# Layer 2's input weights split during layer 1's MLP and kept in DRAM scratch

## The chip, the cores and the metric

The kernel runs on one core of a Trainium2 chip. The metric is the device time of one execution in microseconds (us). The engines are TensorE (PE, with its weight loads PEld), VectorE (DVE), ScalarE (ACT), GpSimd (POOL) and SyncE (SP), which issues nearly all DMAs from one in-order queue.

## The reference

A decoder trunk of two layers on 512 tokens of width 1024, float32. Each layer is

```
h = rmsnorm(x, g_mix[l])
cq, ckv, kr, aq, ak, av, qi, ki, wi, rq, rk, rv, rg = split(h @ w_in[l])
A: latent attention, 8 heads; q from cq, keys and values from ckv, shared rotary key kr
B: sparse attention, 4 heads; scores of qi, ki, wi choose the top 128 keys of each query
C: retention, 4 heads, group norm, gate by silu(rg)
x = x + concat(o_a, o_b, o_c) @ w_out[l]
x = x + square(relu(rmsnorm(x, g_mlp[l]) @ w_ff1[l])) @ w_ff2[l]
```

with the usual causal masks and rotary embeddings, and a last rmsnorm after layer 2. All products are wanted at about float32 accuracy.

## The kernel before

Activations lie transposed, 128 features on the partitions and 512 tokens along a row. Every product of weights and activations is made of three matmuls: both operands are split into a high half, rounded to the fast float32 format of TensorE, and a low half, the rest; high by high, high by low and low by high are added up in one accumulator (`mm3`; its matmuls are recorded at line 141).

Activations are split as they are made. Weights are split on the way in. `wchunk` loads one tile of 128 output columns (128 x 1024 numbers, 512 KB) into a raw buffer `wr` (four of them, line 196), and `wsplit` makes from each half of it a pair `wh`, `wl` of 128 x 512 (four pairs): the high half by a copy (line 187 on ScalarE, line 189 on GpSimd), the low half by a subtraction (line 209 on VectorE, 211 on GpSimd). Which engine takes which is counted out by `mode`: in a layer's front three of four copies go to ScalarE and one to GpSimd, and the subtractions go to VectorE and GpSimd in turn; in the MLP all copies are ScalarE's and all subtractions VectorE's.

`gemm` is `wchunk` and `product`: 24 matmuls of 512 columns for a tile. The input projection of a layer has 19 such tiles (`win_tile`): 0 for keys of B, the rotary key of A and the index key, 1 and 2 index queries, 3 to 6 retention queries and keys, 7 and 8 the gate, 9 and 10 queries of B, 11 and 12 for ckv, 13 to 18 for cq. The token-major columns (`wtk`) are apart from these. In layer 2 tiles 0 and 1 are begun on one half of the tokens (`early`) while the other half (`late`) still waits for the last of layer 1's MLP.

The order of the front's work is written out by hand in `ORDER`: names of tiles, of attention blocks, and of fillers (`t` for a round of the top-128 selection, lines 734 and 735, `r` for a retention score). Rotary tiles are scaled out of the accumulator on VectorE (`scaled`, line 644) and then swap rows by small DMAs on SP (`rope`, line 302). A scheduler places the instructions of each engine at build time from priorities (`PRI`, `hp`); weights have a high one, selection rounds a low one. At run time each engine, and SP's queue with it, goes through its list in order.

The MLP of a layer takes 32 steps `up(f)`, each a gemm with a tile of w_ff1. After every second one, `prep_first(i)` loads two tiles of w_ff2 (line 426, into the same `wr` buffers), forms sums and differences of them (the down product is computed by a scheme of seven products of half size), stores sums in DRAM (`ws`, line 432), and splits what it needs into `v` and `g` buffers; `mul_first(i - 1)` multiplies what the step before prepared (line 502). After the 32 steps come the other products of the scheme. At the end of layer 1 the new x is stored in DRAM (`xd`, line 1235, eight stores of 256 KB) for the residual of layer 2.

The tags `km` (three buffers) and `pe` (three) belong to the attention of a layer and lie idle in its MLP.

Of the kernel before, what the change touches and what calls it, by code (L numbers as in the profile page):

```python
# [10 lines left out]
F32 = mybir.dt.float32  # L11
FR = mybir.dt.float32r
BF = mybir.dt.bfloat16
AF = mybir.ActivationFunctionType
# [3 lines left out]
P = 128  # L18
T = 512
# [6 lines left out]
PEB = 3  # L26
# [3 lines left out]
WB = 4  # L30
WRB = 4
# [40 lines left out]
def trunk_kernel(ctx, tc, xT, gains, win, wtk, wuq, wukv, wout, wff1, wff2, tabs, cf, cb, outT):  # L72
    nc = tc.nc
# [4 lines left out]
    dp = ctx.enter_context(tc.tile_pool(name="dp", bufs=1, space=bass.MemoryType.DRAM))  # L78
# [4 lines left out]
    def hp(k):  # L83
        return tc.high_priority(PRI[k]) if PRI[k] else nullcontext()

    def nm(s):
        count["n"] += 1
        return f"{s}_{count['n']}"

    def S(tag, bufs, shape=None, dt=F32):  # L90
        return sb.tile(shape or [P, T], dt, tag=tag, bufs=bufs, name=nm(tag))
# [33 lines left out]
    def mm_ps():  # L125
        return pp.tile([P, T], F32, tag="mm", bufs=3, name=nm("mm"))
# [7 lines left out]
    def R(ap):  # L134
        return ap.bitcast(F32)
# [7 lines left out]
    def mm3(out, ah, al, bh, bl, start, stop):  # L143
        mm(out, ah, bh, start, False)
        mm(out, ah, bl, False, False)
        return mm(out, al, bh, False, stop)
# [33 lines left out]
    def gcol(i):  # L180
        return gn[:, i : i + 1]
# [11 lines left out]
    def wchunk(src, width, parts=2):  # L193
        with hp("w"):
            raw = S("wr", WRB, [P, 1024])[:, :width]
            nc.sync.dma_start(raw, src)
            return wsplit(raw, width, parts)
# [17 lines left out]
    def product(ch, kk, acts, cols=slice(0, T), out=None):  # L215
        out = mm_ps() if out is None else out
        per = len(kk) // len(ch)
        for j, k in enumerate(kk):
            ah, al = acts[k]
            h, l = ch[j // per]  # L220
            js = slice(j % per * P, j % per * P + P)
            order[j] = mm3(out[:, cols], h[:, js], l[:, js], ah[:, cols], al[:, cols], j == 0, j == len(kk) - 1)
        return out

    def gemm(wsrc, kk, acts, raw=None):
        parts = 2 if len(kk) > 2 else 1
        ch = wchunk(wsrc, len(kk) * P, parts) if raw is None else wsplit(raw, len(kk) * P, parts)
        return product(ch, kk, acts)
# [86 lines left out]
    k8 = list(range(8))  # L315
# [29 lines left out]

    ws = [[dp.tile([P, 2, 2, T], F32, name=f"ws{l}_{j}") for j in range(KP // 2)] for l in range(DEPTH)]
    early, late = slice(256, 512), slice(0, 256)

    def half_squares(xv, n, cols):
        t = [g_(F32, [P, 2, 256]) for _ in range(2)]  # L350
        for i in range(2):
            nc.scalar.activation(t[i], xv[2 * n + i][:, :, cols], AF.Square)
        nc.vector.tensor_add(t[0], t[0], t[1])
        return t[0]
# [55 lines left out]
    def mlp(l, xv, u, rb, nxt):  # L410
# [109 lines left out]

        first = {}
        forms = {}

        def mul_first(i):
            for b, (wh, wl, fh, fl) in zip("167", forms.pop(i)):
                mul(packed(first[b]), (wh, wl), (fh, fl), i)

        for f in range(4 * KD):
            up(f)
            if f % 2:  # L530
                i = f // 2
                forms[i] = prep_first(i)
                if i == 0:
                    first.update({"1": [sc_ps(), sc_ps()], "6": [sc_ps(), o_ps()], "7": [o_ps(), mm_ps()]})
                elif i < KP - 1:
                    mul_first(i - 1)
        p3 = [mm_ps(), mm_ps()]
        o3 = packed(p3)
        for i in range(2):
# [68 lines left out]
    for l in range(DEPTH):  # L608
# [3 lines left out]
        if l == 0:  # L612
            u = [make_u(x[k], gcol(G0 + G_MIX + k)) for k in range(KD)]
            ss = S("ss", 1)
            for k in range(KD):
                s = g_() if k else ss
                if SQP[k] == "p":
                    nc.gpsimd.tensor_mul(s, x[k], x[k])
                else:
                    with after("uh"):  # L620
                        nc.scalar.activation(s, x[k], AF.Square)
                if k:
                    with after("ul"):
                        nc.vector.tensor_add(ss, ss, s)
            rtok = tiny(4, "rtok", 2)
            nc.vector.tensor_copy(rtok, stats(ss, 1024))
            rb = g_()
            bcast(rtok, rb)
        else:
            u, rtok, rb = nxt.u, nxt.rtok, nxt.rb  # L630
            for n in (0, 1):
                ch = wchunk(win[l, n], 1024)
                begun[n] = ch, product(ch, k8, u, early)
            nxt.finish(xp, late, sums)

        def win_tile(n, raw=None):
            if n in begun:
                ch, out = begun[n]
                return product(ch, k8, u, late, out)
            return gemm(win[l, n], k8, u, raw)  # L640

        def scaled(ps, z):
            with hp("e"):
# [516 lines left out]
        for step in ORDER.split():  # L1160
            name, num = step.rstrip("0123456789"), step[len(step.rstrip("0123456789")) :]
            n = int(num or 0)
# [64 lines left out]
        u = [make_u(x[k], gcol(G0 + G_MLP + k)) for k in range(KD)]  # L1227
# [123 lines left out]
```

## Time and profile before

| | |
|---|---|
| median of three runs | 1395.73 us (1391.5 to 1395.9) |
| the profiled execution | 1398.68 us, span 1396.9 us |
| TensorE busy, mean clock | 1326.8 us (95%), 0.976 |
| VectorE busy | 1103.2 us (79%) |
| ScalarE busy | 666.2 us (48%) |
| GpSimd busy | 331.6 us (24%) |
| DMA moved | 197.56 MB |

Layer 1's front runs from 0 to about 320 us, its MLP from about 366 to 705 us; layer 2's front from 705 to about 1006, its MLP from 1048 to the end. A span is from the first to the last instruction; the time of an execution holds some microseconds more around it. In the rows "out<-in" names the buffers written and read, "x14" counts instructions, and the numbers behind the bar are busy time in us, mean of one in ns, and the idle time of the engine just ahead, with what ended it. In the views by stretch the number in brackets counts instructions, and the DMA columns are the share of the DMA engines' time and the GB/s they moved.

### The profile page before, as it was taken

The page shows a single profiled execution, that of the slowest core. Times are in us where ns is not written, and L with a number is a line of the kernel's source. Part 1 is how long each engine was busy: PE and PEld are TensorE (multiplying, and loading weights), DVE is VectorE, ACT ScalarE, POOL GpSimd, SP SyncE. Part 2 cuts the span into 40 slices and gives each one's busy share as a digit, 9 for nine tenths or more (in the row PEclk, how much of TensorE's full clock was granted, in tenths as well). Part 3 has the DMA queues.
Part 4 walks back from the last instruction along what each step waited for, and adds up shares of the span by engine and source line. Part 5 has one row for each costly group of instructions (what it writes and reads, how often), then busy time and mean ns, then how long its engine had stood idle before and what let it go on. Part 6 is the DMA issues. An engine that isn't in the chain of part 4 may idle for free. (4 is left out here: it accounts for less than half of the span.)

```text
span 1396.9 us, 20211 instructions
## 1 busy us (share of the span) xinstructions
PE 1326.8 (95%) x7304; PEld 1102.9 (79%) x7304; DVE 1103.2 (79%) x1843; ACT 666.2 (48%) x1179; POOL 331.6 (24%) x337
## 2 busy tenths in 40 slices
PE   7889988989999999999999999898999999999997
PEld 5767775757788888899988777566778888888997
DVE  6789998887677767788658999878767776777875
ACT  3343443676344344455535345357844444445652
POOL 4446752424100000000034666334240000000000
PEclk9999999999999999999999999999999999999998
DMA  6457522302355554556546671231035555554652
GB/s 218 99 162 183 157 64 70 113 16 63 123 192 171 183 174 154 180 180 215 178 143 188 192 181 52 77 100 46 16 121 163 164 179 178 161 180 151 209 184 78
DMA packets 75780, 197.56 MB, mean 141 GB/s; under 512 B 8960, under 2 KB 13792, under 8 KB 75680
## 3 DMA queue, kind: packets, MB, share of 16 engines
q1 hardware_dynamic: 74528, 195.22, 45.6%
q8 instruction: 58, 0.95, 0.3%
q10 hardware_dynamic: 1152, 1.05, 0.2%
q14 instruction: 42, 0.34, 0.1%
HBM read 155.68 MB, written 20.97 MB: 126 GB/s over the span
## 5 line engine op out<-in xcount | busy, mean ns | idle before, releaser
L141 PE MATMUL mm<-u,wh 128*128 128x512 f32 (+1 forms) x1776 | 561.5, 396 | 1.6 <-DVE u L284 1.2
L141 PEld LDWEIGHTS mm<-u,wh 128*128 128x128 f32 x1776 | 332.7, 190 | 77.4 <-DVE u L284 2.6
L141 PE MATMUL mm<-u,wl 128*128 128x512 f32 (+1 forms) x888 | 351.0, 395 | 3.9 <-DVE wl L209 3.9
L187 ACT ACTIVATE wh<-wr 128x512 fp32r<-128x512 f32 (+2 forms) x247 | 149.8, 611 | 315.8 <-PE mm L141 197.3
L209 DVE TENSOR_TENSOR wl<-wr,wh 128x512 fp32r<-128x512 f32 (+2 forms) x208 | 153.5, 739 | 89.6 <-ACT wh L187 87.3
L211 POOL TENSOR_TENSOR wl<-wr,wh 128x512 fp32r<-128x512 f32 (+2 forms) x80 | 104.7, 1309 | 443.3 <-ACT wh L187 423.7
L141 PEld LDWEIGHTS mm<-u,wl 128*128 128x128 f32 x888 | 168.8, 190 | 43.4 <-DVE wl L209 4.8
L489 DVE TENSOR_TENSOR u<-wr,u 128x1024 fp32r<-128x1024 f32 x54 | 65.8, 1221 | 25.1 <-ACT u L488 24.7
L141 PE MATMUL o<-p,v 128*128 128x512 f32 (+2 forms) x316 | 83.4, 370 | 1.8 <-POOL p L138 1.3
L488 ACT ACTIVATE u<-wr 128x1024 fp32r<-128x1024 f32 x54 | 57.1, 1058 | 53.3 <-PE o L502 14.0
L431 DVE TENSOR_TENSOR sm<-wr 128x512 f32<-128x512 f32 x64 | 44.5, 695 | 36.3 <-DMA wr<-in_wff 36.3
L502 PEld LDWEIGHTS sc<-g,v 128*128 128x128 f32 x576 | 70.3, 188 | 2.9
L502 PE MATMUL sc<-g,v 128*128 128x256 f32 x576 | 71.0, 277 | 0.0
L141 PEld LDWEIGHTS o<-p,v 128*128 128x128 f32 x316 | 52.4, 198 | 12.8 <-DVE p L138 4.1
L419 DVE SCALAR_TENSOR_TENSOR g<-mm,g 128x512 f32<-128x512 f32 x64 | 44.1, 688 | 23.0 <-PE mm L141 22.8
L138 DVE TENSOR_TENSOR p<-pe,p 128x512 fp32r<-128x512 f32 (+2 forms) x78 | 46.5, 623 | 12.0 <-POOL p L189 9.9
L189 POOL TENSOR_SCALAR p<-pe 128x512 fp32r<-128x512 f32 (+1 forms) x46 | 35.1, 767 | 74.2 <-ACT pe L1082 72.6
L735 DVE MATCH_REPLACE8 g<-m,g 128x512 f32<-128x512 f32 (+2 forms) x96 | 51.4, 539 | 0.0
L734 DVE MAX8 m<-g 128x8 f32<-128x256 f32 (+2 forms) x96 | 50.3, 547 | 0.2
L435 ACT ACTIVATE v<-wr 128x1024 fp32r<-128x1024 f32 x32 | 34.1, 1066 | 33.3 <-DVE wr L433 33.1
L189 POOL TENSOR_SCALAR wh<-wr 128x512 fp32r<-128x512 f32 (+3 forms) x41 | 29.8, 726 | 82.9 <-PE mm L141 57.6
L141 PE MATMUL sc<-u,qk 97*128 97x512 f32 (+5 forms) x192 | 46.7, 358 | 2.4 <-ACT pe L1082 2.4
(299 smaller groups left out, 2742.0 us busy)
## 6 DMA issues: line engine op xcount, KB each, us to landing
wr<-in_wff SPq DMA_DIRECT2D x160, 512.0 KB
wr<-in_win SPq DMA_DIRECT2D x37, 512.0 KB
ws<-sm SPq DMA_DIRECT2D x32, 512.0 KB
wr<-ws SPq DMA_DIRECT2D x32, 512.0 KB
tab<-in_tabs SPq DMA_DIRECT2D x20, 512.0 KB
wr<-in_wout SPq DMA_DIRECT2D x16, 512.0 KB
p<-p SPq DMA_DIRECT2D x40, 128.0 KB
wr<-in_wuq SPq DMA_DIRECT2D x12, 384.0 KB
```

The source lines that it names most:

```text
L138: (nc.vector if eng == "v" else nc.gpsimd).tensor_tensor(out, a, b, op=op)
L141: return nc.tensor.matmul(out, lhsT, rhs, start=start, stop=stop)
L187: nc.scalar.activation(out, src, AF.Copy)
L189: nc.gpsimd.tensor_scalar(out, src, 1.0, 1.0, op0=ALU.mult, op1=ALU.mult)
L209: nc.vector.tensor_sub(lo, rc, R(hi))
L211: nc.gpsimd.tensor_sub(lo, rc, R(hi))
L431: nc.vector.tensor_add(sm[:, h], w[0], w[1])
L488: nc.scalar.activation(wh, t, AF.Copy)
L489: nc.vector.tensor_sub(wl, t, R(wh))
L502: nc.tensor.matmul(outs[m][0], a[:, m * P : m * P + P], b, start=i == 0 and outs[m][1] and n == 0, stop=i == KP - 1 and n == 2, skip_group ...
L734: nc.vector.max(m8, accs[j])
L735: nc.vector.match_replace(out=accs[j], in_to_replace=m8, in_values=accs[j], imm_value=GONE)
```

## The change

The 19 input tiles of layer 2 are split in layer 1. A function `halve` loads a tile's raw weights into a `wr` buffer, makes the high halves on ScalarE and the low halves on VectorE in buffers of the tags `km` and `pe`, and stores them in DRAM tiles of their own, 256 KB each, four for a tile. It is called 19 times, spread over the steps f = 2 to 29 of layer 1's MLP. In layer 2 `halved` takes the place of `wchunk`: four loads of 256 KB go straight into the two pairs `wh`, `wl`. Layer 1's own input tiles and all other weights stay as they were.

```diff
--- before.py
+++ after.py
@@ -345,6 +345,29 @@
 
     ws = [[dp.tile([P, 2, 2, T], F32, name=f"ws{l}_{j}") for j in range(KP // 2)] for l in range(DEPTH)]
     early, late = slice(256, 512), slice(0, 256)
+    NWIN = 19
+    halves = [[[dp.tile([P, T], F32, name=f"hl{n}_{c}_{i}") for i in range(2)] for c in range(2)] for n in range(NWIN)]
+
+    def halve(n):
+        raw = S("wr", WRB, [P, 1024])
+        nc.sync.dma_start(raw, win[1, n])
+        for c in range(2):
+            rc = raw[:, c * T : c * T + T]
+            hi, lo = S("km", 3, None, FR), S("pe", PEB, None, FR)
+            nc.scalar.activation(hi, rc, AF.Copy)
+            nc.vector.tensor_sub(lo, rc, R(hi))
+            for t, d in zip((hi, lo), halves[n][c]):
+                nc.sync.dma_start(d, R(t))
+
+    def halved(n):
+        with hp("w"):
+            res = []
+            for c in range(2):
+                t = S("wh", WB, None, FR), S("wl", WB, None, FR)
+                for s, d in zip(halves[n][c], t):
+                    nc.sync.dma_start(R(d), s)
+                res.append(t)
+            return res
 
     def half_squares(xv, n, cols):
         t = [g_(F32, [P, 2, 256]) for _ in range(2)]
@@ -520,6 +543,7 @@
 
         first = {}
         forms = {}
+        done = [0]
 
         def mul_first(i):
             for b, (wh, wl, fh, fl) in zip("167", forms.pop(i)):
@@ -534,6 +558,10 @@
                     first.update({"1": [sc_ps(), sc_ps()], "6": [sc_ps(), o_ps()], "7": [o_ps(), mm_ps()]})
                 elif i < KP - 1:
                     mul_first(i - 1)
+            if l == 0 and 2 <= f < 30 and (f - 1) * NWIN // 28 > (f - 2) * NWIN // 28:
+                halve(done[0])
+                done[0] += 1
+        assert l or done[0] == NWIN, done
         p3 = [mm_ps(), mm_ps()]
         o3 = packed(p3)
         for i in range(2):
@@ -629,7 +657,7 @@
         else:
             u, rtok, rb = nxt.u, nxt.rtok, nxt.rb
             for n in (0, 1):
-                ch = wchunk(win[l, n], 1024)
+                ch = halved(n)
                 begun[n] = ch, product(ch, k8, u, early)
             nxt.finish(xp, late, sums)
 
@@ -637,7 +665,7 @@
             if n in begun:
                 ch, out = begun[n]
                 return product(ch, k8, u, late, out)
-            return gemm(win[l, n], k8, u, raw)
+            return product(halved(n), k8, u) if l else gemm(win[l, n], k8, u, raw)
 
         def scaled(ps, z):
             with hp("e"):
```

## Rows read from the trace of the kernel before

**Rows 1.** Busy time by stretch: us and instructions by engine; clock; DMA
```profile
366.00:606.00 240.00, 240.00 (x1316) 205.50 (x1316) 176.94 (x287) 104.49 (x165) 0.00 (x0) 1.00 0.52 166
...
705.00:750.00 45.00, 42.83 (x278) 39.27 (x277) 29.64 (x52) 16.78 (x38) 21.10 (x22) 1.00 0.60 171
...
750.00:910.00 160.00, 149.38 (x651) 113.50 (x650) 151.30 (x311) 71.86 (x144) 87.54 (x87) 0.97 0.47 134
...
910.00:1006.00 96.00, 88.30 (x447) 62.98 (x445) 79.13 (x131) 66.97 (x139) 31.91 (x39) 0.95 0.15 48
```

**Rows 2.** VectorE's instructions by line and shape, 750 to 910 us
```profile
L209 DVE TENSOR_TENSOR wl<-wr,wh 128x512 fp32r<-128x512 f32 x14 | 11.6, 830 | 0.0
...
L138 DVE TENSOR_TENSOR p<-p,tab 128x512 f32<-128x512 f32 x7 | 7.6, 1091 | 0.0
...
L138 DVE TENSOR_TENSOR p<-p 128x512 f32<-128x512 f32 x7 | 6.1, 867 | 0.8 <-POOL p L138 0.8
...
L232 DVE TENSOR_TENSOR g<-p,g 128x512 fp32r<-128x512 f32 x5 | 5.1, 1027 | 0.0
```

**Rows 3.** The same view, VectorE in layer 1's MLP, 400 to 600 us
```profile
L209 DVE TENSOR_TENSOR wl<-wr,wh 128x512 fp32r<-128x512 f32 x50 | 34.4, 688 | 29.3 <-ACT wh L187 29.1
```

**Rows 4.** The same view, GpSimd and ScalarE, 705 to 910 us
```profile
L211 POOL TENSOR_TENSOR wl<-wr,wh 128x512 fp32r<-128x512 f32 x18 | 26.1, 1447 | 23.8 <-ACT wh L187 23.1
...
L187 ACT ACTIVATE wh<-wr 128x512 fp32r<-128x512 f32 x28 | 17.6, 630 | 26.1 <-PE mm L141 18.3 <-PE o L141 4.3 <-DVE p L232 3.3
```

**Rows 5.** Instructions of line 734: durations, first and last start
```profile
L734 DVE MAX8 m<-g x96: 402/547/695, 90.6 to 910.2; 128x8 f32<-128x256 f32 x32, 128x8 f32<-128x384 f32 x32, 128x8 f32<-128x512 f32 x32
```

**Rows 6.** Chain that ended last, two steps of an MLP: start, us
```profile
1071.51 11.20 PE mm L141 x48
```

**Rows 7.** TensorE's matmuls by shape, 750 to 910 us, first and last of 40
```profile
L141 PE MATMUL mm<-u,wh 128*128 128x512 f32 x250 | 79.9, 396 | 0.0
...
L141 PE MATMUL sc<-u,qk 97*128 97x384 f32 x1 | 0.3, 338 | 0.0
```

**Rows 8.** Timeline of layer 1's MLP: SP, VectorE, TensorE's weight loads
```profile
490.07 6.59 SPq L426 DMA_DIRECT2D wr<-in_wff  x2
...
493.81 0.69 DVE L431 TENSOR_TENSOR sm<-wr 128x512 f32<-128x512 f32 x1 [1.09 <-DMA wr<-in_wff]
...
501.64 0.68 DVE L450 TENSOR_TENSOR g<-g,g 128x512 fp32r<-128x512 f32 x1
...
509.20 2.24 PEld L502 LDWEIGHTS sc<-g,v 128*128 128x128 f32 x18
```

**Rows 9.** Waits of SP's queue in layer 1's MLP
```profile
SPq L426 <- DVE wl L209: 134.9, 30, 7.6
```

**Rows 10.** Busy time by stretch, where the DMA queue is full
```profile
10.00:12.00 2.00, 1.52 (x7) 0.90 (x6) 2.00 (x3) 2.00 (x4) 0.44 (x1) 1.00 1.03 409
...
706.00:707.00 1.00, 1.00 (x11) 1.00 (x10) 1.00 (x2) 1.00 (x4) 1.00 (x1) 1.00 1.09 414
```

**Rows 11.** Waits of SP's queue, 705 to 910 us: total, times, longest
```profile
SPq L196 <- DVE wl L209: 42.6, 10, 10.1
...
SPq L302 <- DVE p L644: 16.0, 3, 8.8
...
SPq L302 <- DVE g L727: 9.2, 2, 8.6
...
SPq L768 <- ACT g L187: 6.8, 2, 5.3
```

**Rows 12.** Timeline between the layers: SP, GpSimd, TensorE
```profile
702.40 6.17 SPq L1235 DMA_DIRECT2D xd<-x  x8
...
705.00 0.62 POOL L189 TENSOR_SCALAR wh<-wr 128x512 fp32r<-128x512 f32 x1 [3.00 <-PE sc L502]
...
709.55 0.36 PE L141 MATMUL mm<-u,wh 128*128 128x256 f32 x1
```

## The prediction

> **What bounds the kernel now.** I read first the busy time of each engine in stretches of layer 2's front (its 19 input projection tiles and the attention that follows) and of layer 1's MLP, where the new work is put [rows 1]. In the up half of the MLP (366 to 606 us) TensorE is busy without a gap: 240.0 of 240 us at clock 1.00, with VectorE at 176.9, ScalarE at 104.5, GpSimd at nothing and the DMA engines at a share of 0.52. That stretch is bound by TensorE, and the rest of it is cover. In the front it is the other way round. From 750 to 910 us VectorE is busy 151.3 of 160 us. TensorE's 149.4 there is not its need: records are stretched where it waits inside a product. At full rate the chain of waits shows 48 matmuls of 512 columns in 11.20 us [rows 6], 0.233 us each. Taking the columns of all 40 forms between 750 and 910 [rows 7] at that rate (290,064 columns / 512 x 0.233) gives 132 us; so TensorE has some 28 us in hand there, and VectorE 8.7.
>
> What VectorE does there is the selection of the top 128 keys (rounds of max and match-replace, at low priority, so that they fill every gap) and the low halves of the weight splits, the rope and the attention's own splits. The last round of the selection starts at 910.2 us [rows 5], and the masks for the sparse attention wait for it. From 910 to 1006 us VectorE is at 79.1 of 96 and the chain passes from engine to engine. So I take the stretch 750 to 910 as VectorE's, and its end as the point that moves.
>
> **Removed.** Each input tile is one load of 512 KB into a raw buffer, two copies for the high halves (three of four on ScalarE, the fourth on GpSimd) and two subtractions for the low halves (one on VectorE, one on GpSimd). All go from layer 2. VectorE: 14 subtractions of 128x512 lie in 750 to 910, 11.6 us at 830 ns each [rows 2]. Two or three of these may belong to other weights (the 128x512 shape is shared with the output projection), which would take 1.7 to 2.5 us off; on the other side the win tiles before 750 have theirs too, but there VectorE is at 29.6 of 45 us [rows 1] and they are worth nothing. I keep 11.6 and carry the 2.5 to the range. ScalarE's 28 copies (17.6 us) [rows 4] lie on an engine busy 71.9 of 160 us: nothing.
>
> GpSimd: 18 subtractions of 1447 ns [rows 4] go, and they slow VectorE. The same subtraction takes VectorE 688 ns in the MLP, where GpSimd stands still [rows 3], and 830 ns here. The other operations with two operands that stay show the same: rope's products 1091, its sums 867, the splits 1027 ns [rows 2]. Over 688 ns that is 7 x 0.40 + 7 x 0.18 + 5 x 0.34 = 5.8 us of delay. GpSimd is busy 87.5 us there; of the 18 some 14, the same number as VectorE's, lie in the stretch, 20 us, and with them a copy in four tiles or so: about a quarter of it goes. A quarter of 5.8 is 1.5 us. Bounds: nothing, and 5.8.
>
> The Trainium skill says of this, in "SBUF — State Buffer", section "Who interferes with whom", that a VectorE operation with two SBUF inputs and a GpSimd operation that reads SBUF shut each other out for the whole instruction. This case's rows agree that there is a delay, 142 ns a subtraction; by the rule the most that could come back is the whole of the removed GpSimd time, and the sum would be lower by some 19 us. That is a rival below.
>
> Sum of the front's gain: 11.6 + 1.5 = 13.1 us, well inside TensorE's 28.
>
> **Moved into layer 1's MLP.** For each tile: one load of 512 KB, two ScalarE copies, two VectorE subtractions, four stores of 256 KB, all DMAs on SP's queue. 38 subtractions x 0.688 [rows 3] are 26.1 us, and VectorE goes from 176.9 to 203.1 of 240 us; 38 copies x 0.63 [rows 4] are 23.9, and ScalarE goes to 128.4. Both stay under TensorE, which gets nothing new. Bytes: 19 x (0.524 + 4 x 0.262) = 29.9 MB over 28 of the 32 up steps (210 us) are 142 GB/s on the 166 there [rows 1], 308 together. The stretches with full queues show what is to be had: 409 GB/s with loads alone, and 414 while the eight stores of x run beside loads [rows 10]. So 308 fits, by a quarter.
>
> What this lies beside is latency. SP already waits 134.9 us of this stretch for a raw buffer that VectorE has to give back [rows 9]: all four are always full, and a load goes out when one comes free. A second-MLP-matrix load issued at 490.07 is what VectorE waits for at 493.81, so 3.7 us from issue to use; its products' operands are ready at 502.3 (501.64 plus 0.68) and TensorE takes them at 509.20 [rows 8]: 6.9 us in hand. A new raw buffer is held 3.7 + 2 x (0.63 + 0.69) = 6.3 us, 120 us for all 19, of 4 x 240 that exist. If loads are put off by less than 6.9 us, TensorE does not see it. I take the cost as nothing; if that cover is gone, it is the slower rival's price below. Stores: eight take SP 6.17 us [rows 12], 0.77 each, and 76 of them 59 us, in place of waits.
>
> **Added in layer 2.** Each tile becomes four loads of 256 KB, straight into the split buffers. These are four pairs deep, two tiles; the raw buffers had let four more tiles run ahead. A pair feeds 12 matmuls for each half tile, 24 a tile: 2.8 us. A pair freed by TensorE is needed three halves later, 8.4 us where tiles follow each other. Two issues (0.4 each, estimated from the issues of 0.33 to 0.77) and at most the 3.7 us of the larger load make 4.5; what is left, 3.9 us, is what SP may be held up by another wait at its head. In 705 to 910 us SP's longest waits are 10.1, 8.8, 8.6 and 5.3 us [rows 11]. The first is for raw buffers, and goes; what stands above 3.9 in the others is 4.9, 4.7 and 1.4, together 11 us, if every one fell just before a needed load and TensorE had no slack; none, if they fell elsewhere. TensorE has slack; I take 3 us.
>
> The Trainium skill speaks against this part: "DMA: Bandwidth & Descriptors", section "Anatomy of one DMA", fits a transfer (on the GpSimd path) as 2.0 us and its bytes at 436 GB/s, so 2.6 us for each of four against 3.2 for the one before. Taken one after the other that is 10.4 us a tile, nearly twice the 5.6 us in which TensorE eats it, and some 91 us over 19 tiles. The rows do not show it one after the other: transfers of one queue run beside each other, at 414 GB/s with a store every 0.77 us [rows 10, 12].
>
> At the passage between layers the second tile's buffers come free at 705.0 (the copy on GpSimd waits for TensorE until then), SP is taken up with the eight stores of x from 702.40 to 708.57, and TensorE goes on with the next product at 709.55 [rows 12]. Loads ahead of the stores land at about 705.0 + 0.8 + 3.7 = 709.5, in time; behind them at 708.6 + 4.5 = 713. I take the middle, 2 us; bounds 0 and 4.
>
> **Sum.** 13.1 - 3 - 2 = 8.1 us less than the profiled execution's own time: 1398.7 (its span is 1396.9) becomes 1390.6. That execution lies 3 us above the median of the runs shown, so beside them 1395.7 - 8.1 = 1387.6. Its own range: low, 18.9 (5.8 instead of 1.5 and both costs nothing), 1378; high, 11.6 - 2.5 - 4 - 4, about 1394.
>
> **Rivals.**
> *Late weights.* The loads wait on SP behind rope swaps and TensorE stops at the tiles; the gain is eaten. For it: the prefetch shrinks from six tiles to two, and SP waits long [rows 11]. Against: TensorE's 28 us. At 11 + 4 us of loss it is 13.1 - 15 = 2 us slower than now, near 1397; where the swaps in turn are held up behind loads that wait for TensorE, 5 us more, 1402.
> *The MLP pays.* One mechanism: a new tile's load and its stores stand in SP's queue ahead of a load of the second MLP matrix, which goes out only when the halves are there: 6.3 us and four issues of 0.77, 9.4 in all, against the 6.9 in hand [rows 8]. From there on TensorE waits, 2.5 us for each. All 19: 47 us, half of them: 24. At half it is 24 - 8 = 16 us slower, 1412. Against: the four buffers, of which one more load in five needs one, and the order in SP's queue, which can put the stores later.
> *The port gives back more.* If the removed GpSimd time came back in full, VectorE would need 151.3 - 11.6 - 20 = 120 us, less than TensorE's 132; the gain stops at 28 - 5 = 23 us, 1373. Against: a delay of only 142 ns a subtraction.
>
> **Chances.** The forecast 0.43; the port 0.07; late weights 0.31, of it 0.22 about even (1392 to 1400) and 0.09 slower; the MLP 0.19. A measurement of this kernel tells apart about 0.3%, 4 us. Faster 0.50, same 0.22, slower 0.28. The range 1375 to 1411 leaves out most of the port's case and the upper half of the MLP's.
>
> **What would show it.** Right: the stretch that answers to 366 to 606 keeps its 240 us with VectorE near 203; VectorE in the front loses its weight subtractions, its rope products fall below 1091 ns; the last max starts some 8 us sooner, counted from the end of layer 1. Wrong: gaps of TensorE in layer 1's MLP ended by a load or by VectorE; waits of TensorE for a DMA into the split buffers in the front; or a selection that ends as late as now though VectorE has less to do, which would mean that it was not VectorE that set 910.

## The result and the profile after

The changed kernel takes 1410.19 us (median of five executions; 1405.77 to 1412.32), the kernel before 1395.82 us in the same rounds (1391.5 to 1398.0). The ratio of the means is 1.0096, 95% interval 1.0072 to 1.0120: slower by about 1%, where 0.6% faster was forecast. A sixth execution of the changed kernel took 2095 us at a mean granted clock of 0.555 and is left out. The profiled execution took 1406.02 us (span 1403.7).

The busy time by stretch, for the rows that answer to [rows 1]:

```profile
366.00:606.00 240.00, 233.80 (x1247) 196.38 (x1246) 187.93 (x304) 110.27 (x190) 0.00 (x0) 1.00 0.85 282
...
705.00:750.00 45.00, 43.09 (x303) 39.90 (x302) 20.71 (x46) 12.54 (x29) 6.22 (x6) 1.00 0.58 183
750.00:910.00 160.00, 150.64 (x667) 116.57 (x666) 139.98 (x307) 59.81 (x125) 65.95 (x72) 0.98 0.68 193
910.00:1006.00 96.00, 88.01 (x475) 63.51 (x475) 79.73 (x129) 64.09 (x139) 32.94 (x41) 0.98 0.18 59
```

TensorE got 1247 matmuls done in the stretch in which it had done 1316, and is no longer without gaps; the DMA share went from 0.52 to 0.85. How long a stage took is read better from its own landmarks. The instructions of four lines, first and last start: the exits of layer 1's up steps (VectorE takes a step's product out of the accumulator), the top-128 rounds of both layers, the stores of x, and the additions to x behind layer 2's output projection:

```profile
L442 DVE SCALAR_TENSOR_TENSOR g<-mm,g x32: 677/682/692, 369.4 to 614.6; 128x512 f32<-128x512 f32 x32
...
L762 DVE MAX8 m<-g x96: 398/548/697, 91.2 to 874.3; 128x8 f32<-128x256 f32 x32, 128x8 f32<-128x384 f32 x32, 128x8 f32<-128x512 f32 x32
...
L1263 SPq DMA_DIRECT2D xd<-x x8: 319/398/1040, 714.3 to 721.4; - x8
...
L1252 DVE TENSOR_TENSOR x<-x,mm x8: 672/680/689, 1018.1 to 1050.3; 128x512 f32<-128x512 f32 x8
```

The first and the last of these in the kernel before:

```profile
L419 DVE SCALAR_TENSOR_TENSOR g<-mm,g x32: 682/691/692, 370.7 to 601.3; 128x512 f32<-128x512 f32 x32
...
L1224 DVE TENSOR_TENSOR x<-x,mm x8: 678/688/690, 1008.8 to 1042.7; 128x512 f32<-128x512 f32 x8
```

The up steps took 230.6 us and now take 245.2. From the first exit to the first store of x, nearly the whole MLP, it was 331.7 us and is now 344.9: 13.2 us more, and 0.96% of the kernel is 13.4. (The spans of the two profiled executions lie only 6.8 us apart; in the changed one what lies ahead of the first exit, layer 2's front and what follows it each ran one to three us shorter.) The up steps are a sharp measure where nothing disturbs them: in the four kernels below that put at most one of the new splits into layer 1's MLP (e2, e3, e4, e16), they take 230.6 to 230.7 us. Where they are disturbed, single traces scatter: the changed kernel and e1 have the same MLP part, and so have e14 and e15, and they differ by 2 and 4 us in it.

The rest of layer 2 tells the other half. The last selection round, counted from the first store of x, came at 910.2 - 702.4 = 207.8 us [rows 5, 12] and now comes at 874.3 - 714.3 = 160.0: 48 us sooner. The first addition behind layer 2's output projection starts at 1018.1 now, 303.8 us after that store; before it was at 1008.8, 306.4 us after. So of 48 us of lead 2.6 were left, and even these can't be told from scatter: in the twelve kernels below whose layer 2 is that of the kernel before, this stage takes 304.5 to 311.3 us, and in e2, whose layer 2 is the changed one, 309.9. The busy time of the stage, in the kernel before, the changed kernel and e2:

```profile
702.40:1008.80 306.40, 285.48 (x1404) 220.33 (x1403) 263.10 (x497) 157.92 (x324) 140.56 (x147) 0.97 0.39 113
...
714.30:1018.10 303.80, 282.96 (x1415) 219.49 (x1415) 244.30 (x481) 140.84 (x298) 107.65 (x120) 0.98 0.50 147
...
696.70:1006.60 309.90, 289.59 (x1415) 222.50 (x1415) 244.11 (x482) 141.15 (x298) 107.86 (x120) 0.96 0.49 144
```

The differences go with TensorE's granted clock, 0.97, 0.98 and 0.96: a hundredth of it is some 3 us of this stage (an estimate, 0.01 of 306 us).

What was waited for in the stretch of the up steps (366 to 620 us), TensorE's weight loads, ScalarE and SP's queue; total, times, longest:

```profile
PEld mm L141 <- ACT wh L187: 8.0, 7, 1.8
PEld mm L141 <- DVE wl L209: 3.0, 7, 0.4
...
ACT km L357 <- DMA wr<-in_win: 42.2, 15, 5.8
ACT wh L187 <- DMA wr<-in_wff: 22.5, 13, 3.9
...
ACT wh L187 <- PE mm L141: 5.0, 4, 2.2
...
SPq L360 <- ACT km L357: 33.6, 21, 3.2
...
SPq L360 <- DVE pe L358: 17.9, 13, 2.4
```

The line to look at is the copies' wait for TensorE. ScalarE's waits in the kernel before, 366 to 606 us:

```profile
ACT wh L187 <- PE mm L141: 60.2, 40, 2.4
ACT wh L187 <- DMA wr<-in_wff: 34.2, 14, 3.4
```

There the high-half copies waited 60.2 us for a pair that TensorE still used: the weights were ready ahead of it. Now that wait is 5.0 us, the lead is gone, ScalarE stands 64.7 us before loads (42.2 of them at the new copies), and TensorE waits for halves. The chain that ended last, 400 us on:

```profile
400.56 5.56 DMA wr<-in_win
406.12 0.02 issue
406.14 0.02 ACTq L357
406.16 0.04 issue
406.20 0.09 ACT km L357
```

A load that took 3.7 us from issue to use [rows 8] takes 5.6 here, and the chain goes through it and the new copy. How that copy blocks ScalarE is in its timeline:

```profile
458.04 0.62 ACT L472 ACTIVATE g<-g 128x512 fp32r<-128x512 f32 x1
464.20 1.15 ACT L357 ACTIVATE km<-wr 128x512 fp32r<-128x512 f32 x2 [5.55 <-issue]
465.26 0.61 ACT L443 ACTIVATE qk<-g 128x512 f32<-128x512 f32 x1
469.78 1.15 ACT L187 ACTIVATE wh<-wr 128x512 fp32r<-128x512 f32 x2 [3.90 <-DMA wr<-in_wff]
```

SP's timeline has the issue of a new raw load at 459.34 us and the next at 475.67, so the copies at 464.20 are of the first, 4.9 us on. ScalarE stood for 5.55 us (this row names no releaser) with the square of an up step (L443) behind, then stood 3.90 us more for the load of another weight.

### The profile page after: what moved, and what is told of

The parts are those of the page before. It is cut to its first block, busy times and chain, and to the rows that moved or that the text cites. A ratio compares the mean times of both kernels' runs of the same rounds, so it can differ in the third digit from the quotient of the medians.

```text
span 1403.7 us, 20471 instructions
## 1 busy us (share of the span) xinstructions
PE 1325.9 (94%) x7302; PEld 1100.3 (78%) x7304; DVE 1105.1 (79%) x1862; ACT 662.5 (47%) x1189; POOL 297.2 (21%) x308
## 3 DMA queue, kind: packets, MB, share of 16 engines
q10 hardware_dynamic: 1152, 1.05, 0.2%
## 4 chain that ended last, share of the span: by engine, by line
PE 59%; DVE 18%; DMA 10%; issue 6%; ACT 5%; POOL 1%; SPq 1%; POOLq 0%; DVEq 0%; ACTq 0%
PE mm L141 34%; PE sc L525 8%; PE sc L141 6%; DMA wr<-in_wff 5%; PE mm L525 4%; PE o L525 4%; DMA wr<-in_win 3%; PE o L141 2%; DVE wl L209 2%; DVE p L138 2%; DVE g L755 1%; DVE g L763 1%; DVE m L762 1%; DVE v L459 1%; ACT wh L187 1%
## 5 line engine op out<-in xcount | busy, mean ns | idle before, releaser
L187 ACT ACTIVATE wh<-wr 128x512 fp32r<-128x512 f32 (+3 forms) x219 | 129.0, 604 | 228.4 <-PE mm L141 141.9
L209 DVE TENSOR_TENSOR wl<-wr,wh 128x512 fp32r<-128x512 f32 (+3 forms) x189 | 137.7, 739 | 82.9 <-ACT wh L187 80.9
L211 POOL TENSOR_TENSOR wl<-wr,wh 128x512 fp32r<-128x512 f32 (+3 forms) x61 | 78.5, 1288 | 459.5 <-DMA p<-p 373.7
L525 PE MATMUL o<-g,v 128*128 128x256 f32 x384 | 49.7, 280 | 0.0
L525 PEld LDWEIGHTS o<-g,v 128*128 128x128 f32 x384 | 47.0, 191 | 0.0
```

The lines of the kernel that those rows point to most:

```text
L187: nc.scalar.activation(out, src, AF.Copy)
L209: nc.vector.tensor_sub(lo, rc, R(hi))
L211: nc.gpsimd.tensor_sub(lo, rc, R(hi))
L525: nc.tensor.matmul(outs[m][0], a[:, m * P : m * P + P], b, start=i == 0 and outs[m][1] and n == 0, stop=i == KP - 1 and n == 2, skip_group ...
```

## The experiments

Each ratio is to the kernel before, run beside it. "Up" is the up steps of layer 1's MLP in the profiled execution, "start" the first exit in them, "MLP" the time from that exit to the first store of x. "Lead" is the time for which ScalarE's weight copies waited for TensorE from 366 to 606 us. "Up" ends with VectorE's last exit, which can come some us behind the product on TensorE; where "up" and "MLP" differ, the second tells what was lost.

| run | ratio (95%) | start | up | MLP | lead |
|---|---|---|---|---|---|
| before | 1 | 370.7 | 230.6 | 331.7 | 60.2 |
| changed kernel | 1.0096 (1.0072, 1.0120) | 369.4 | 245.2 | 344.9 | 5.0 |
| e1 MLP part | 1.0099 (1.0071, 1.0127) | 369.2 | 241.4 | 342.6 | 4.6 |
| e9 loads only | 1.0105 (1.0067, 1.0143) | 369.0 | 243.5 | 346.4 | 4.6 |
| e10 splits only | 1.0026 (1.0002, 1.0049) | 378.1 | 229.5 | 332.0 | 45.2 |
| e13 one buffer held | 1.0049 (1.0028, 1.0069) | 365.3 | 235.6 | 338.7 | 3.3 |
| e5 e1, no stores | 1.0061 (1.0040, 1.0082) | 368.7 | 237.3 | 337.3 | 4.6 |
| e6 own raw buffers | 1.0108 (1.0085, 1.0132) | 378.9 | 237.4 | 339.3 | 10.5 |
| e11 e6, no stores | 1.0092 (1.0060, 1.0123) | 380.4 | 232.2 | 333.2 | 59.3 |
| e12 e6, splits later | 1.0103 (1.0062, 1.0144) | 376.2 | 235.4 | 336.8 | 13.7 |
| e14 e12, fixed places | 1.0067 (1.0043, 1.0092) | 369.3 | 239.1 | 340.9 | 11.8 |
| e17 e14, no stores | 1.0082 (1.0056, 1.0108) | 370.8 | 235.0 | 339.2 | 21.2 |
| e15 whole change, e14's MLP | 1.0061 (1.0041, 1.0082) | 367.5 | 235.0 | 337.2 | 10.0 |
| e18 e15, stores from ScalarE | 1.0068 (1.0048, 1.0088) | 369.8 | 238.1 | 340.7 | 6.3 |

**The two parts apart (e1, e2).** The MLP part alone, with layer 2 as before:

```diff
-                ch = halved(n)
+                ch = wchunk(win[l, n], 1024)
...
-            return product(halved(n), k8, u) if l else gemm(win[l, n], k8, u, raw)
+            return gemm(win[l, n], k8, u, raw)
```

> Layer 1's MLP as changed (19 tiles split and stored), layer 2's input tiles loaded raw and split as in the kernel before; nothing is left out of the result. If the two parts of the change add up and the MLP pays by itself: its up steps take about 245 us as in the changed kernel against 231, and the kernel is 12 to 16 us slower than before. If the MLP pays only together with what layer 2 does (a shifted order): under 5 us slower.

And the front alone:

```diff
-                for s, d in zip(halves[n][c], t):
+                for s, d in zip(halves[0][c], t):
...
-                halve(done[0])
+                if done[0] == 0:
+                    halve(0)
```

> Only one tile is split and stored in layer 1's MLP, and all 19 input tiles of layer 2 load that one from DRAM, so layer 2's values are those of wrong weights; loads, waits and order of layer 2 are those of the changed kernel. If the front's gain is the 2.6 us seen between the stores of x and the output projection: 1 to 5 us faster than before. If the MLP's delay had also spoiled the front: 8 to 13 us faster.

e1: 1.0099, the whole loss. e2: 0.9984 (0.9960, 1.0007). The parts add up to the whole, +0.99% and -0.16% against +0.96%, and the front that was to bring 8 us brings 2.2 with an interval that holds zero.

**How much the front could give (e3, e4, e16).** e3 takes loads, splits and waits of the 19 tiles away altogether:

```diff
-                halve(done[0])
+                pass
...
+            fx = x0fix
+            res_.append([(fx, fx)] * 2)
...
-                ch = halved(n)
+                ch = resident()
...
-            return product(halved(n), k8, u) if l else gemm(win[l, n], k8, u, raw)
+            return product(resident(), k8, u) if l else gemm(win[l, n], k8, u, raw)
```

> Layer 2's 19 input tiles are multiplied with one resident buffer as high and low half: no load, no split and no wait for weights, and no work in layer 1's MLP; layer 2's values are wrong. If VectorE's work sets the front (the prediction's theory): 13 us faster or more. If late weights eat the gain: also 10 us or more, while the run with loads gets 3. If the written order and its chains set the front: within 2 us of the run with loads, 3 to 6 us faster than before.

e4 is the kernel before with half of layer 2's selection rounds; e16 is e3 and e4 together.

```diff
-                fill_top.append((top_round, j))
+                fill_top.append((top_round if l == 0 or _ % 2 == 0 else lambda j: None, j))
```

> The kernel before with every second round of layer 2's top-128 selection left out (24 rounds of 1.1 us on VectorE, 27 us; the selection keeps 64 keys). If VectorE's work up to the last round sets the end of the front: 15 to 25 us faster. If the written order and its chains set it: under 5 us faster.

> Layer 2's input tiles with one resident buffer as weights (no load, split or wait), and every second round of its selection left out; the result is wrong. Alone they gave 0.55% and 0.2%. If VectorE's work set the front, 40 us of it are gone: 25 us faster or more. If the written order and its chains set it: 6 to 11 us faster, the sum of the two or less.

e3: 0.9945 (0.9918, 0.9971). e4: 0.9980 (0.9958, 1.0002). e16: 0.9944 (0.9926, 0.9962). The busy time of layer 2's front in e16:

```profile
697.00:997.00 300.00, 283.37 (x1418) 219.57 (x1417) 221.95 (x408) 140.40 (x296) 106.29 (x119) 0.97 0.31 84
```

The kernel before has VectorE at 263.10 us over the 306 us of the same stage. Some 40 us of VectorE's work are gone, half of the selection and the splits of all 19 tiles, and the kernel is no faster than with the splits alone gone. In this order of work, whatever is done to these weights can give about 0.55%, some 8 us (0.29 to 0.82% by e3's interval). The quantity of VectorE's work does not set this stage.

**What in layer 1's MLP costs (e5, e7 to e10, e13).** Stores away (e5); both halves made on GpSimd, which stands still there (e7); stores issued from GpSimd's queue (e8). All three are e1 and an edit in `halve`; in this order:

```diff
-            for t, d in zip((hi, lo), halves[n][c]):
-                nc.sync.dma_start(d, R(t))
```

```diff
-            nc.scalar.activation(hi, rc, AF.Copy)
-            nc.vector.tensor_sub(lo, rc, R(hi))
+            copy_fr(hi, rc, "p")
+            nc.gpsimd.tensor_sub(lo, rc, R(hi))
```

```diff
-                nc.sync.dma_start(d, R(t))
+                nc.gpsimd.dma_start(d, R(t))
```

> As the MLP-only kernel (layer 2 splits its own tiles), but the 76 stores are left out: the loads, copies and subtractions in layer 1's MLP stay. If the stores cost it (SP waits for the halves ahead of each store, or the store traffic makes loads late): within 3 us of the kernel before. If the raw buffers or the copies at the head of ScalarE cost it: still 10 us or more slower.

> As the MLP-only kernel, but the high and low halves are made on GpSimd, which has nothing else to do there; ScalarE and VectorE have nothing new in their queues. If a new copy at the head of ScalarE's queue, waiting for its load, holds up the splits behind it: within 4 us of the kernel before. If raw buffers or stores cost it: as slow as before or slower, since GpSimd holds a raw buffer for 2 x 0.7 + 2 x 1.3 us.

> As the MLP-only kernel, but the 76 stores are issued from GpSimd's queue. The bytes are the same; SP issues and waits for loads only. If SP's waits for the halves ahead of the stores cost it: within 4 us of the kernel before. If the bytes of the stores make the loads late: still 10 us or more slower.

e5: 1.0061, up steps 237.3 us: without one store most of the loss is still there. e7: 1.0328 (1.0305, 1.0351), up 273.1. e8: 1.0264 (1.0241, 1.0287), up 268.0; its new copies wait 62.8 us for their loads, up to 7.0 at a time. Neither takes the load off what matters; one reading, not tried apart, is that both hold the raw buffers longer.

So load and split were tried apart. e9 keeps the 19 raw loads, each released by a copy of one column; e10 keeps the 38 copies and 38 subtractions and takes them from resident tiles. In `halve`, e9 and then e10:

```diff
-        for c in range(2):
-            rc = raw[:, c * T : c * T + T]
...
-                nc.sync.dma_start(d, R(t))
+        nc.gpsimd.tensor_copy(S("pe", PEB)[:, 0:1], raw[:, 0:1])
```

```diff
-        raw = S("wr", WRB, [P, 1024])
-        nc.sync.dma_start(raw, win[1, n])
+        raw = xv[n % 4].rearrange("p h n -> p (h n)")
...
-            for t, d in zip((hi, lo), halves[n][c]):
-                nc.sync.dma_start(d, R(t))
```

> Layer 2 as in the kernel before; in layer 1's MLP only the 19 raw loads are left, each into one of the four raw buffers, which is given back once GpSimd has copied one column of it; no halves are made or stored. If the loads by themselves (a buffer of the four, a place in SP's queue, 10 MB) cost the MLP its time: 5 to 12 us slower than before. If it is the waits that hang on them (ScalarE's copies, stores): within 3 us.

> Layer 2 as in the kernel before; in layer 1's MLP only the 38 copies on ScalarE and 38 subtractions on VectorE are left, taken from tiles of x that lie in SBUF, so nothing waits for a load and nothing is stored. If the added 26 us on VectorE and 24 on ScalarE lengthen the MLP by themselves: 3 us slower or more. If only the waits for DMAs do: within 3 us of the kernel before, up steps 231 us.

The exits of the up steps in e9, then in e10:

```profile
L436 DVE SCALAR_TENSOR_TENSOR g<-mm,g x32: 682/684/692, 369.0 to 612.5; 128x512 f32<-128x512 f32 x32
```

```profile
L439 DVE SCALAR_TENSOR_TENSOR g<-mm,g x32: 681/686/692, 378.1 to 607.6; 128x512 f32<-128x512 f32 x32
```

This pair decides most. The loads alone, with almost no work behind them, cost 1.05% and 13 us of the up steps; the splits alone cost these steps nothing (229.5 us). But not all of e10's splits lie in the steps. Its copies:

```profile
L356 ACT ACTIVATE km<-x x38: 613/617/635, 334.8 to 438.0; 128x512 fp32r<-128x512 f32 x38
```

Of the 38 copies 15, and of the 38 subtractions 13, start ahead of the first exit at 378.1, from layer 1's output projection on, and the others are done by 439 us. So e10 shows that some two dozen splits, closer together than the change has them, pass under TensorE; it doesn't show it for all 38. e10's 0.26% lies outside the steps: they begin later, at 378.1 (its profiled execution, 1411.75 us, lies 9 us above its median, so 378.1 overstates it).

A load needs bandwidth, a place in SP's queue and one of four buffers. e13 is the kernel before with no new transfer: one of the four is held from step 2 to step 29 and not used.

```diff
+            if l == 0 and f == 2:
+                kept = S("wr", WRB, [P, 1024])
+                nc.gpsimd.memset(kept[:, 0:1], 0.0)
+            if l == 0 and f == 29:
+                with after("uact"):
+                    nc.scalar.activation(S("pe", PEB)[:, 0:1], kept[:, 0:1], AF.Copy)
```

> The kernel before, with one of the four raw buffers held from step 2 to step 29 of layer 1's MLP; no load, no store and no split is added. If the MLP needs all four buffers (the loads-only kernel lost 13 us in the up steps with nothing but a fifth user of them): up steps 5 us or more above 231 and the kernel 0.3% slower or more. If it was the added loads themselves, and not the buffer they take: up steps within 2 us of 231.

```profile
ACT wh L187 <- DMA wr<-in_wff: 92.7, 27, 4.8
...
ACT wh L187 <- PE mm L141: 3.3, 1, 3.3
```

These are ScalarE's waits from 366 to 600 us. A held buffer costs 0.49% and 7.0 us of the MLP by itself, and the copies' lead over TensorE is gone, 3.3 us where there were 60.2. (Its last pair of second-matrix loads in the steps waits 5.5 us for the release itself; thirteen ahead of it wait 66 us for VectorE, as much each, so the pace is the same.) Loads that share the buffers cost more than that (e9), and there the transfers are real.

**Own raw buffers (e6, e11, e12, e14, e17).** If it were only the four buffers, other ones should heal it. In e6 the raw tiles go to the buffers of the tag `tab`, which are free there, and the calls are spread over steps 2 to 27; e11 is e6 without stores; in e12 a tile's splits and stores are written one call after its load. e6, and what e12 adds:

```diff
-        raw = S("wr", WRB, [P, 1024])
+        raw = S("tab", TABB, [P, 2, T]).rearrange("p h n -> p (h n)")
```

```diff
+        if waiting:
+            finish_halve(*waiting.pop())
+        if n < NWIN:
...
+            waiting.append((n, raw))
```

> As the MLP-only kernel, but the new raw tiles go into the two table buffers, idle in the MLP until its step 28, instead of the four raw buffers that the MLP's own loads need; the 19 calls are spread over steps 2 to 27. If the shortage of raw buffers costs it: within 4 us of the kernel before. If the stores or ScalarE's order cost it: still 10 us or more slower.

> As the MLP-only kernel with the new raw tiles in the two table buffers, and without the stores. Each alone took the up steps of the profiled runs from 241 to 237 us. If the two causes are separate and add up: up steps about 233, within 4 us of the kernel before. If they are one and the same wait (whichever is taken away, the other holds the loads up): about 237 still.

> As the MLP-only kernel, the raw tiles in the table buffers, and each tile's copies, subtractions and stores are written one call later than its load (steps 2 to 27), so that the load has a step or two to land before anything asks for it. If the cost is queues standing at an instruction whose load has not landed: within 4 us of the kernel before, and no wait of ScalarE's new copies for a load. If the stores' place in SP's queue or their bytes cost it: as with own buffers, some 12 us slower.

None is better: 1.0108, 1.0092, 1.0103. But the loss has moved. In e11 the up steps take 232.2 us with a lead of 59.3, nearly as before, and begin at 380.4. Its new loads on SP, first and last issue, and ScalarE's timeline ahead of the MLP:

```profile
L353 SPq DMA_DIRECT2D tab<-in_win x19: 327/328/539, 208.0 to 406.9; - x19
...
363.00 0.63 ACT L357 ACTIVATE km<-tab 128x512 fp32r<-128x512 f32 x1 [1.96 <-DMA tab<-in_win]
...
368.10 1.15 ACT L357 ACTIVATE km<-tab 128x512 fp32r<-128x512 f32 x2 [2.29 <-DMA tab<-in_win]
...
370.08 0.63 ACT L273 ACTIVATE g<-x 128x512 f32<-128x512 f32 x1 [0.32 <-DVE x L1250]
```

With a free buffer nothing ties a load or a split to its step. The scheduler put the first loads of e11 at 208 us, in layer 1's attention, 16 of 19 ahead of the first exit, and copies among the norm ahead of the MLP (L273), where ScalarE stands at their loads. So e11's up steps hold three of the loads, and those of e6 and e12 ten; none of the three shows what 19 loads cost the MLP with buffers of their own. e14 therefore ties them, and all 19 loads lie in the steps again: the load behind a store of sums, the copies behind a step's square, the subtractions behind an exit.

```diff
+            with after("usp"):
+                nc.sync.dma_start(raw, win[1, n])
...
+            with after("uact"):
+                nc.scalar.activation(hi, rc, AF.Copy)
+            with after("udve"):
+                nc.vector.tensor_sub(lo, rc, R(hi))
```

> As the MLP-only kernel, but the raw tiles lie in the two table buffers, copies and subtractions come a call later than the load, and each is placed behind the MLP step that it is written after (behind its square on ScalarE, its product's exit on VectorE, its store of sums on SP), so that they can't move ahead into layer 1's output projection as they did with own buffers. If raw buffers, the stores' and copies' places and the move ahead were the whole cost: start of the MLP and up steps as before (231 to 233), the kernel within 4 us of before. If the bytes of the stores cost it in any order: up steps 235 or more.

> As the MLP part with table buffers and fixed places, without the 76 stores; layer 2 splits its own tiles. If what was left of the MLP's cost (up steps 235 to 239, kernel 0.67% slower) is the stores: up steps 231 to 233 and the kernel within 0.3% of before. If it is the loads' traffic or the copies: up steps still 235 or more.

The start is back (369.3, 370.8), and 0.67% and 0.82% are left. The busy time of e17 by stretch:

```profile
366.00:426.00 60.00, 60.00 (x320) 50.79 (x320) 47.03 (x80) 29.43 (x49) 0.00 (x0) 1.00 0.62 200
...
546.00:606.00 60.00, 60.00 (x336) 51.63 (x334) 51.28 (x84) 30.07 (x51) 0.00 (x0) 1.00 0.57 184
...
612.00:615.00 3.00, 1.11 (x4) 0.91 (x5) 3.00 (x7) 3.00 (x7) 0.00 (x0) 0.70 0.22 67
615.00:618.00 3.00, 3.00 (x16) 3.00 (x15) 2.10 (x2) 1.47 (x2) 0.00 (x0) 0.50 0.98 338
618.00:621.00 3.00, 3.00 (x20) 3.00 (x19) 2.10 (x3) 1.39 (x2) 0.00 (x0) 0.66 0.88 304
```

Its timeline at the end of the steps, TensorE's last up product and what follows, and VectorE's last exit:

```profile
601.07 0.40 PE L141 MATMUL mm<-u,wl 128*128 128x512 f32 x1
...
612.25 0.39 PE L534 MATMUL sc<-g,v 128*128 128x256 f32 x1 [3.30 <-ACT g L479]
614.28 3.99 PE L534 MATMUL sc<-g,v 128*128 128x256 f32 x17 [1.64 <-DVE g L480]
...
605.82 0.68 DVE L451 SCALAR_TENSOR_TENSOR g<-mm,g 128x512 f32<-128x512 f32 x1
```

TensorE is full to 606 us, and its last up product ends at 601.5, 230.7 us behind the first exit, as before. The 4.4 us by which "up" is longer are VectorE's: its list is late, and it takes the last exit 4.3 us behind the product. The operands of the next products are made behind that exit, and there TensorE stands, 3.3 us for ScalarE's and 1.6 us for VectorE's part. Its granted clock then falls to 0.50, the lower of its two levels (1.2 GHz): 17 matmuls take 3.99 us. In the kernel before the clock is 1.00 there, and 18 take 2.36:

```profile
607.92 2.36 PE L502 MATMUL sc<-g,v 128*128 128x256 f32 x18
```

The 4.9 us of standing and some 3 us lost to the clock (an estimate: the busy times from 612 to 621 us times what their clocks lack of 1.00) account for the 7.5 us by which e17's MLP is longer, of 8.2 us in its span (1405.1 against 1396.9). e13 ends in the same way: the exit 2.8 us behind the product, 1.4 and 1.6 us of standing, 17 matmuls in 4.00 us. What makes VectorE late by the end of the steps stays open.

**The whole change with that MLP part (e15, e18).** e15 is the changed kernel with e14's edits; e18 issues its stores from ScalarE's queue.

```diff
-                nc.sync.dma_start(d, R(t))
+                nc.scalar.dma_start(d, R(t))
```

> The whole change with the MLP part of the run beside it, nothing left out. If the MLP's cost is gone and the front gives what the front-only kernel gave: 1 to 5 us faster than before. If the MLP still pays: slower by what that run shows, less 2 us.

> The whole change with table buffers and fixed places, the 76 stores issued from ScalarE's queue; nothing left out. If the stores cost by their place in SP's queue (a store there waits for its half, and the MLP's loads behind it with it): up steps 231 to 233 and the kernel 0 to 5 us faster than before, by the front's gain. If their bytes cost it, or their issues on ScalarE (76 of some 0.6 us): still 4 us slower or more.

1.0061 (1.0041, 1.0082) and 1.0068 (1.0048, 1.0088): some 5 us better than the change as it was, by the middles (the intervals overlap), and still slower than the kernel before. No version tried that does the whole work beats it.

## Why the prediction was wrong

**The step that failed first: "If loads are put off by less than 6.9 us, TensorE does not see it. I take the cost as nothing".** The term that was put at nothing measured 13.2 us in the changed kernel's MLP and 13.8 us in e1 by its ratio. The sums of engine work held in the main: VectorE was to rise from 176.9 to 203.1 us in the stretch and rose to 187.9, since of a stretched stage less falls into 240 us (304 instructions, where 287 and 38 new ones make 325), and in e10 two dozen of the splits passed under TensorE at no cost to the up steps. What failed is the slack. The 6.9 us were read at one load of the second matrix. What TensorE waits for in the changed kernel's up steps are mostly halves of the first one's tiles, 8.0 and 3.0 us, and the lead of their copies was far smaller: 60.2 us over 40 waits, 1.5 us each. It was used up and not built up again: 3.3 to 5.0 us of it are left in e1, e5, e9, e13 and the changed kernel alike.

Two arguments stood behind the step. One is the raw buffers, 120 us of the 4 x 240 that exist. The row that spoke against it was on the table, SP's 134.9 us of waiting for a buffer [rows 9]: all four were always full, so a new user takes the place of a load that would have gone out. e13 shows that one buffer fewer costs 7.0 us of the MLP with no new transfer, e9 that 19 loads in these buffers cost 14.7. The other is "So 308 fits, by a quarter", measured against stretches of one and two us. [rows 1] has 166 GB/s at a share of 0.52, which is 319 at a full share (an estimate), and the changed kernel moved 282 at 0.85: there was next to no room. How the cost divides between buffer, traffic and SP's queue is not shown. e17, with buffers of its own and no stores, still pays 7.5 us, so the shared buffers are not all of it; its fixed places without loads, and new loads from another queue than SP's, were not tried.

**The rival that came** is *the MLP pays*: 1412 forecast at a chance of 0.19, 1410.2 measured, which also lies just inside the upper end of the range, 1411. That the number is so near is luck: the rival added 24 us of cost and 8 of gain, and some 14 and 2 came (e1, e2). Its mechanism held in part only. It made a new tile's load and its stores in SP's queue responsible, ahead of a load of the second matrix. The stores do hold SP, 51.5 us, but without them 0.61% remains of 0.99% (the intervals just overlap), and with raw buffers of their own the stores made no difference that can be told (e14, e17). The loads by themselves cost as much as the whole part (e9). The new copies in ScalarE's list, ahead of the steps' own work, were priced in no rival; e11 shows ScalarE standing at copies whose data is not there, outside the up steps.

**The second step that failed: "I take the stretch 750 to 910 as VectorE's, and its end as the point that moves."** The end did move, 48 us instead of 8, and nothing came of it. The prediction named this sign itself, in another form: a selection that ends late though VectorE has less to do. What happened is the reverse, a selection that ends early though nobody waits for it. A busy share of 151 in 160 us was read as a bound, but much of it was selection rounds of low priority that fill every gap: they stretch over the time there is. Taking out half of them (e4) gave 0.2% with an interval that holds zero (up to 0.42%); taking them out on top of all weight work (e16) gave nothing. What does set the 304 us from the stores of x to the output projection is shown by exclusion only: not VectorE's quantity of work, and not the weights beyond 0.55%. TensorE's own columns there, at 0.233 us for 512, come to some 248 of the 306 us in the kernel before (an estimate from its matmuls by shape), so TensorE's work, with its clock of 0.96 to 0.98, is the larger part of the stage. For the rest, the order written out by hand and the passing of results between engines are what is left; which chain it is stays open.

**Point by point of the front.** VectorE's weight subtractions of 128x512 fell from 14 to 1, as said, and the operations that stay became shorter. The answer to [rows 2], in the stretch that begins as far behind the MLP (762 to 922 us):

```profile
L138 DVE TENSOR_TENSOR p<-p,tab 128x512 f32<-128x512 f32 x7 | 7.0, 995 | 1.1 <-DMA p<-p 1.1
L138 DVE TENSOR_TENSOR p<-p 128x512 f32<-128x512 f32 x7 | 4.7, 676 | 1.2 <-POOL p L138 1.2
...
L232 DVE TENSOR_TENSOR g<-p,g 128x512 fp32r<-128x512 f32 x5 | 3.7, 747 | 0.9 <-ACT g L187 0.9
L209 DVE TENSOR_TENSOR wl<-wr,wh 128x512 fp32r<-128x512 f32 x1 | 1.0, 1002 | 0.5 <-ACT wh L187 0.5
```

The relief is 7 x 0.096 + 7 x 0.191 + 5 x 0.280 = 3.4 us where 1.5 was taken: right in kind, less than half of what came, and inside the bounds of 0 and 5.8. GpSimd's busy time in the stretch fell from 87.5 to 63.5 us, so VectorE got back about a seventh of the time removed. The Trainium skill, "SBUF — State Buffer", section "Who interferes with whom", calls the ports that VectorE shares with GpSimd an exclusive lock. The prediction took from it that at most the whole of the removed time could come back; here the rows show a part. All of this is saved work on an engine that did not set the time, so 13.1 us of gain became the 2.2 of e2.

**The late weights** cost less than priced. TensorE's waits for the direct loads in layer 2's front:

```profile
PEld mm L141 <- DMA wl<-hl: 1.0, 4, 0.3
...
PEld mm L141 <- DMA wh<-hl: 0.4, 2, 0.3
```

1.4 us where 3 were taken (11 at the bound, worked out from four of SP's waits; the same view has two more, of 5.9 and 5.8 us). SP's longest wait from 705 to 910 us, 10.6 us, did not stop them. That e3, with no loads at all, is 0.39% faster than e2 may say that they cost some 5 us in another way, through SP's queue or the DMA share; the intervals of the two overlap (0.9960 and 0.9971), so this is not settled. The 2 us of the passage between layers can't be told apart either: the stage from the last exit to the first store of x takes 99.7 us against 101.1, and what follows it is in the 303.8.

## What to carry to other kernels

A buffer ring that is always full has no room to share, whatever its mean occupancy: the sign is the queue's own wait for it, and the test is to hold one buffer and do nothing with it. Buffers of one's own are no cure by themselves: here they let work slip ahead of its stage, and tied to its stage it still cost. Slack has to be read at the wait that ends next, not at a roomy one. An engine that is 95% busy with filler of low priority need not be a bound; take out some of the filler before counting on what relieves the engine. And run the two halves of such a move by themselves first: here one run each would have shown a cost of 1% against a gain of some 0.2%.

## What the runs showed of the hardware

Three things had not been expected. With its 76 stores of 256 KB issued from the queue of an otherwise idle GpSimd (e8), the MLP part had up steps of 268.0 us; with the same stores from SP's queue (e1) it had 241.4, and the kernel before 230.6. From ScalarE's queue (e18) no difference to SP's can be told: 238.1 us, where two kernels with that MLP part and SP's queue have 239.1 and 235.0. Two dozen splits on VectorE and ScalarE cost TensorE nothing in e10, while the MLP part with its splits on an idle GpSimd (e7) had up steps of 273.1 us. And a short stand of TensorE costs more than itself: in e17, after 3.3 and 1.6 us of standing with one matmul between, the granted clock was 0.50, and 17 matmuls of 256 columns took 3.99 us where 18 had taken 2.36.
